# Attention tiles of a hybrid layer: one PSUM row per score tile, one bias-and-minimum pass, one cast and one subtraction, 1/sum moved into the gate

## The chip, the cores and the metric

The kernel runs on one core of one Trainium2 chip. The core has five engines that run their own instruction streams: TensorE (PE; its weight loads are listed apart as PEld), VectorE (DVE), ScalarE (ACT), GpSimd (POOL) and SyncE (SP, which here only issues DMAs). The metric is the time of one execution on the device in microseconds (us). Before the change the median of three runs is 1415.39 us (1412.73 to 1422.43).

## The reference, cut to what matters

One layer over 2048 latent tokens (a grid of 32 rows by 64 columns) and 256 context tokens, width 1024. After a norm and one input projection, half of the width goes through neighbourhood attention (8 heads of 64), the other half through retention (4 heads of 128); both are gated and projected out. The change is in the attention:

```python
s_loc = einsum('bhrqd,bhrkd->bhrqk', qr, kg) * scale + bias     # local window, 8 x 16 keys per query
s_loc = where(mask, s_loc, -inf)
s_ctx = einsum('bhrqd,bhcd->bhrqc', qr, k_ctx) * scale           # 256 context keys, no bias
p = softmax(concatenate([s_loc, s_ctx], axis=-1), axis=-1)       # one softmax over both
o = einsum('bhrqk,bhrkd->bhrqd', p_loc, vg) + einsum('bhrqc,bhcd->bhrqd', p_ctx, v_ctx)
y_na = merge(o) * silu(na_g)
```

All inputs are float32. Products are made in two float32r halves: a value is cast to a high part, and the difference is the low part.

## The kernel before, in words

**Stages.** Until about 560 us the kernel normalises, projects and writes q, k, v and the gates to DRAM scratch (qS, kS, vS, gS). From about 562 to 1062 us run the attention tiles, with the rest of the projection (for the retention) mixed in as filler. Then come the retention's states, scans and the output projection.

**The tiles.** There are 8 heads with 16 tiles each (NT = 128): 4 row blocks i by 4 column blocks j. A tile has 128 queries (8 rows by 16 columns), a window of 12 or 16 rows by 24 or 32 columns of local keys (nk = 288, 384 or 512) and 256 context keys (LC).

**One step of the loop (L958-L1013).** The step t works on three tiles, in this order of issue on all engines:

1. tick() runs deferred stores and other deferred work (L133). A store issued with store() goes out one or more ticks later, in this stage on ACT's DMA queue.
2. s_mm(t): TensorE, four matmuls, local scores into a PSUM tile pl (two buffers), context scores into one half of a PSUM tile pc that two tiles share (L742, L743; order pl, pc, pl, pc).
3. fill(part[0]): filler, one step is 3 or 6 matmuls of the projection (L351, L362). A unit of it ends with an evacuation on ACT and DVE, for the rotary units on DVE with tables that were loaded in the middle of the unit (L405, L435; DVE L412-L414, L448-L450).
4. s_min(t): DVE, context scores copied with a running minimum (L752), then local scores plus bias and minimum in one custom instruction (L754).
5. p_tr(t-2): TensorE transposes 3 or 4 blocks of local and 2 of context weights into PSUM tiles tl and tcx (L773, L776, one buffer each), ACT casts them into pt in two instructions (L778, L779).
6. s_exp(t): ACT, exponential with the sum accumulated (L759). p_lo(t-2): DVE, the low parts in two subtractions (L786, L787). s_norm(t): DVE reciprocal of the sum (L764), POOL multiplies the whole row by it (L765).
7. fill(part[1]), then pv(t-3): TensorE, weights times values into po (L797, L799), and after each second tile combine: ACT copies 64 partitions of po (L817), DVE adds (L818), POOL makes two adds (L821) and, for the last of a row block of an odd head, the product with the gate (L825), which is stored to yS.
8. fill(part[2]), then loads and bias work for later tiles: the bias tiles (POOL, L719, L722), the gate (L807), q of the next row block (L697), values vt in groups of four image rows (L705, 6 buffers), k and context values of the next head (L683, L686).

**What sets the order.** The order is written out by hand; each engine and each DMA queue runs in that order. SP issues all loads of this stage, one after another. A load waits until the buffer that it fills was used for the last time, and all later loads wait behind it. Two halves of one PSUM bank in one tile are not written and read at the same time: the writer waits for the reader.

Of the kernel before, what the change touches and what calls it, by code (L numbers as in the profile page):

```python
# [18 lines left out]
P = 128  # L19
# [57 lines left out]
def hybrid_kernel(ctx: ExitStack, tc: tile.TileContext, a: dict, out: bass.AP):  # L77
# [12 lines left out]
    yS = [dram.tile([KC, P, L // 2], F32, name=f"yS{u}") for u in range(2)]  # L90

# [512 lines left out]
    psl = pool(pax, "psl", 2, space=PSUM)  # L604
    psc = pool(pax, "psc", 1, space=PSUM)

# [73 lines left out]
    def load_head(h):  # L680
        k2 = kp.tile([P, LT], F32R, name="k2")
        for hl in range(2):
            nc.sync.dma_start(f(k2)[64 * hl:64 * hl + 64, :], kS[h // 2][64 * (h % 2):64 * (h % 2) + 64, hl, :])  # L683
        vh = vS[h // 4][:, h % 4, :]
        vc = kp.tile([P, 2, P], F32R, name="vc")
        nc.sync.dma_start(f(vc), vh[L:, :].rearrange("(n p) d -> p n d", p=P))  # L686
        return dict(k2=k2, vh=vh, vc=vc, nb={}, vt={}, q={})

    def load_e(hd, h):
        hd["e"] = kp.tile([P, 16, 32], F32, name="rpbe")  # L690
# [9 lines left out]
    def load_v(hd, gs):  # L700
        for g in gs:
            vt = kp.tile([P, 4, P], F32R, name="vt", bufs=6)
# [10 lines left out]
    def bias(hd, rt, ct):  # L713
# [7 lines left out]
        t = mp.tile([P, kr, cw], F32, name=f"nb{int(rt == 1)}{ct}")  # L721
        nc.gpsimd.tensor_tensor(t, mcol[:, ct, ec:ec + cw].unsqueeze(1).to_broadcast([P, kr, cw]),  # L722
                                hd["ep"][:, :, ec:ec + cw], ALU.subtract)
        hd["nb"][rt, ct] = t
# [7 lines left out]
    def s_mm(t):  # L732
        h, i, j, kr0, kr, kc0, cw = dims(t)
        hd, nk = heads[h], kr * cw
        if t % 2 == 0:
            tl_st["pc"] = psc.tile([P, 2, LC], F32, name="pc")
        pc = tl_st["pc"][:, t % 2, :]
        pl = psl.tile([P, 512], F32, name="pl")
        kg = hd["k2"][:, :L].rearrange("p (r c) -> p r c", c=GW)
        for hl in range(2):  # L740
            qa = hd["q"][i][:, hl, j * P:(j + 1) * P]
            nc.tensor.matmul(pl[:, :nk], qa, kg[:, kr0:kr0 + kr, kc0:kc0 + cw], start=(hl == 0), stop=(hl == 1))  # L742
            nc.tensor.matmul(pc, qa, hd["k2"][:, L:], start=(hl == 0), stop=(hl == 1))  # L743
        sp = ap_.tile([P, 768], F32, name="sp", bufs=3)
        st = ap_.tile([P, 4], F32, name="stt", bufs=4)
        tl_st[t] = dict(pl=pl, pc=pc, sp=sp, st=st, nk=nk)

    def s_min(t):
        h, i, j = dims(t)[:3]
        T = tl_st[t]  # L750
        sp, st, nk = T["sp"], T["st"], T["nk"]
        nc.vector.tensor_scalar(sp[:, nk:nk + LC], T["pc"], 1.0, None, ALU.mult, ALU.min, accum_out=st[:, 0:1])  # L752
        nb = heads[h]["nb"][RTYPE[i], CTYPE[j]].rearrange("p a b -> p (a b)")
        nc.vector.tensor_tensor_reduce(sp[:, :nk], T["pl"][:, :nk], nb, 1.0, st[:, 0:1], ALU.add, ALU.min, st[:, 1:2])  # L754

    def s_exp(t):
        T = tl_st[t]
        sp, st, n = T["sp"], T["st"], T["nk"] + LC
        nc.scalar.activation(sp[:, :n], sp[:, :n], AF.Exp, bias=st[:, 1:2], scale=-1.0, accum_out=st[:, 2:3])  # L759

    def s_norm(t):
        T = tl_st[t]
        sp, st, n = T["sp"], T["st"], T["nk"] + LC
        nc.vector.reciprocal(st[:, 3:4], st[:, 2:3])  # L764
        nc.gpsimd.tensor_scalar(sp[:, :n], sp[:, :n], st[:, 3:4], 0.0, ALU.mult, ALU.add)  # L765

    def p_tr(t):
# [3 lines left out]
        tl = psl.tile([P, 4, P], F32, name="tl", bufs=1)  # L771
        for g in range(ng_):
            nc.tensor.transpose(tl[:cn, g, :], sp[:, g * cn:(g + 1) * cn], ident)  # L773
        tcx = psc.tile([P, 2, P], F32, name="tcx")
        for g in range(2):
            nc.tensor.transpose(tcx[:, g, :], sp[:, nk + g * P:nk + (g + 1) * P], ident)  # L776
        pt = ap_.tile([P, 6, 2, P], F32R, name="pt")
        nc.scalar.copy(pt[:cn, :ng_, 0, :], tl[:cn, :ng_, :])  # L778
        nc.scalar.copy(pt[:, 4:, 0, :], tcx)  # L779
        T.update(tl=tl, tcx=tcx, pt=pt)  # L780

    def p_lo(t):
        h, i, j, kr0, kr, kc0, cw = dims(t)
        T = tl_st[t]
        pt, ng_, cn = T["pt"], kr // 4, 4 * cw
        nc.vector.tensor_tensor(pt[:cn, :ng_, 1, :], T["tl"][:cn, :ng_, :], f(pt)[:cn, :ng_, 0, :], ALU.subtract)  # L786
        nc.vector.tensor_tensor(pt[:, 4:, 1, :], T["tcx"], f(pt)[:, 4:, 0, :], ALU.subtract)  # L787

    def pv(t):
        h, i, j, kr0, kr, kc0, cw = dims(t)  # L790
        T, hd = tl_st[t], heads[h]
        pt, ng_, cn = T["pt"], kr // 4, 4 * cw
# [5 lines left out]
        for g in range(2):  # L798
            nc.tensor.matmul(po[:, t % 2, :, :], hd["vc"][:, g, :], pt[:, 4 + g, :, :], start=False, stop=(g == 1))  # L799
# [4 lines left out]
    def load_gate(t):  # L804
        h, i = dims(t)[:2]
        gts[t // 4] = ap_.tile([P, 512], F32, name="gt")
        nc.sync.dma_start(gts[t // 4], gS[h // 2][:, i * 512:(i + 1) * 512])  # L807

    def combine(t):
# [6 lines left out]
        tmp = ap_.tile([P, 2, 2, P], F32, name="cmb", bufs=1)  # L816
        nc.scalar.copy(tmp[fin], po[oth])  # L817
        nc.vector.tensor_tensor(tmp[fin], po[fin], tmp[fin], ALU.add)  # L818
        yv = ys[i][fin].rearrange("p (r w c) -> p r w c", r=8, w=4)
        for jj in range(2):  # L820
            nc.gpsimd.tensor_tensor(yv[:, :, 2 * jp + jj, :], tmp[fin, jj, 0, :].rearrange("p (r c) -> p r c", r=8),  # L821
                                    tmp[fin, jj, 1, :].rearrange("p (r c) -> p r c", r=8), ALU.add)
        if h % 2 == 1 and jp == 1:
            gt, y2 = gts.pop(t // 4), ys[i]
            nc.gpsimd.tensor_tensor(gt, y2, gt, ALU.mult)  # L825

            y_put(h // 2, i // 2, (i % 2) * 512, gt, 2)
# [522 lines left out]
```

## Time and profile before

| what | us |
|---|---|
| median of 3 runs (lowest, highest) | 1415.39 (1412.73, 1422.43) |
| span of the profiled execution, first to last instruction | 1413.8 |
| PE busy in that span | 1346.2 (95%) |
| DVE / ACT / POOL busy | 670.2 / 553.4 / 614.5 |
| attention stage, 560 to 1062: PE / DVE / ACT / POOL busy | 469.4 / 351.9 / 281.4 / 335.3 |

The page gives for each engine the time in which it had an instruction in work. A row of the view of waits reads: the waiting engine and its line, what it waited for, the total in us, how often, and the longest. A row of the groups reads: line, engine, operation, output and inputs with their shapes, count, then busy us and mean ns of one, then the idle time just before them and what ended it. SPq and ACTq are the DMA issues of SP and ACT.

### The profile page before, as it was taken

The numbers are of one execution on the slowest core, as the hardware profiler recorded it, in microseconds if no ns is written. First come the engines' busy times: TensorE is split into PE (matmuls) and PEld (weight loads), VectorE is DVE, ScalarE is ACT, GpSimd is POOL, SyncE is SP. The second block draws the span as 40 slices with busy tenths as digits, with TensorE's granted clock in tenths as the row PEclk, the third lists the DMA queues.
The fourth block names the chain that finished last, engine by engine and source line by source line (L and its number), as shares of the span: only waits on it lengthen the run. The fifth ranks groups of instructions, "written<-read, shape, count | busy, mean of one in ns | idle before, by whom it ended". The sixth has DMA issues, their size and how long they took to land.

```text
span 1413.8 us, 23044 instructions
## 1 busy us (share of the span) xinstructions
PE 1346.2 (95%) x8380; PEld 1175.6 (83%) x8380; DVE 670.2 (47%) x1563; ACT 553.4 (39%) x1283; POOL 614.5 (43%) x703
## 2 busy tenths in 40 slices
PE   6989999999999999999899988798999999999997
PEld 2467899988887888998799878598999879888886
DVE  5786111100021131677777767577673644344445
ACT  4454212212212221765466544356563234333332
POOL 4452302112201221676777746477673155454342
PEclk9999999999999999999999999999999999999999
DMA  9543666233244577557557585847436997555433
GB/s 310 168 164 133 215 219 231 92 110 104 90 147 159 202 266 218 141 156 196 158 155 174 162 241 167 227 124 191 134 115 203 295 310 258 188 168 174 154 117 127
DMA packets 203634, 253.20 MB, mean 179 GB/s; under 512 B 13057, under 2 KB 151425, under 8 KB 202498
## 3 DMA queue, kind: packets, MB, share of 16 engines
q1 hardware_dynamic: 168098, 186.98, 45.2%
q10 hardware_dynamic: 35424, 64.76, 12.7%
q8 instruction: 66, 1.08, 0.3%
q14 instruction: 46, 0.38, 0.1%
HBM read 168.86 MB, written 82.84 MB: 178 GB/s over the span
## 4 chain that ended last, share of the span: by engine, by line
PE 73%; DMA 10%; DVE 8%; ACT 3%; POOL 2%; issue 2%; SPq 1%; ACTq 0%; DVEq 0%; POOLq 0%
PE mm L351 24%; PE mm L362 19%; PE mm L1193 11%; PE po L797 2%; PE tl L773 2%; PE pl L742 2%; PE mm L916 2%; DMA t<-in_rot_s_dram 2%; DMA q<-qS 2%; PE pc L743 1%; PE po L799 1%; PE tcx L776 1%; PE mm L295 1%; DMA t<-in_rot_k_dram 1%; PE mm L1105 1%
## 5 line engine op out<-in xcount | busy, mean ns | idle before, releaser
L351 PE MATMUL mm<-hhi,whi 128*128 128x512 f32 x640 | 259.6, 406 | 0.0
L351 PE MATMUL mm<-hlo,whi 128*128 128x512 f32 x640 | 253.4, 396 | 5.6 <-DVE hlo L264 2.2
L351 PE MATMUL mm<-hhi,wlo 128*128 128x512 f32 x640 | 253.3, 396 | 0.3 <-DVE wlo L332 0.3
L362 PE MATMUL mm<-whi,hhi 128*128 128x256 f32 x768 | 224.6, 292 | 0.0
L362 PE MATMUL mm<-wlo,hhi 128*128 128x256 f32 x768 | 216.7, 282 | 2.7 <-POOL wlo L332 2.7
L362 PE MATMUL mm<-whi,hlo 128*128 128x256 f32 x768 | 216.1, 281 | 0.0
L332 POOL TENSOR_TENSOR wlo<-st,whi 128x256 fp32r<-128x256 f32 (+1 forms) x97 | 112.4, 1176 | 225.4 <-ACT whi L330 225.2
L765 POOL TENSOR_SCALAR sp<-sp,stt 128x640 f32<-128x640 f32 (+2 forms) x128 | 103.6, 810 | 105.4 <-DVE stt L764 79.6
L362 PEld LDWEIGHTS mm<-wlo,hhi 128*128 128x128 f32 x768 | 145.0, 189 | 3.4 <-POOL wlo L332 3.3
L351 PEld LDWEIGHTS mm<-hlo,whi 128*128 128x128 f32 x640 | 120.8, 189 | 31.3 <-issue 3.3
L362 PEld LDWEIGHTS mm<-whi,hhi 128*128 128x128 f32 x768 | 145.2, 189 | 1.1
L362 PEld LDWEIGHTS mm<-whi,hlo 128*128 128x128 f32 x768 | 145.3, 189 | 0.0
L351 PEld LDWEIGHTS mm<-hhi,whi 128*128 128x128 f32 x640 | 120.9, 189 | 29.1 <-issue 4.6
L351 PEld LDWEIGHTS mm<-hhi,wlo 128*128 128x128 f32 x640 | 120.5, 188 | 29.4 <-DVE wlo L332 0.7
L759 ACT ACTIVATE sp<-sp,stt 128x640 f32<-128x640 f32 (+2 forms) x128 | 107.9, 843 | 51.8 <-DVE stt L754 51.3
L778 ACT CAST pt<-tl 96x384 fp32r<-96x384 f32 (+3 forms) x128 | 67.9, 531 | 150.6 <-PE tl L773 137.2
L786 DVE TENSOR_TENSOR pt<-tl,pt 96x384 fp32r<-96x384 f32 (+3 forms) x128 | 79.4, 620 | 44.5 <-ACT pt L778 43.8
L1193 PE MATMUL mm<-wor,y 128*128 128x512 f32 x384 | 95.6, 398 | 1.5 <-DVE xt L1202 1.1
L742 PE MATMUL pl<-k,q 128*128 128x384 f32 (+2 forms) x256 | 83.3, 346 | 7.1 <-DMA q<-qS 7.1
L1193 PE MATMUL mm<-won,y 128*128 128x512 f32 x336 | 89.9, 406 | 0.0
L743 PE MATMUL pc<-k,q 128*128 128x256 f32 x256 | 72.1, 286 | 16.8 <-DVE sp L752 16.7
L1193 PEld LDWEIGHTS mm<-wor,y 128*128 128x128 f32 x384 | 69.9, 188 | 17.7 <-issue 3.4
(220 smaller groups left out, 2639.1 us busy)
## 6 DMA issues: line engine op xcount, KB each, us to landing
st<-in_w_in_dram SPq DMA_DIRECT2D x48, 512.0 KB
q<-qS SPq DMA_DIRECT2D x64, 256.0 KB
vS<-o ACTq DMA_DIRECT2D x18, 512.0 KB
k<-kS SPq DMA_DIRECT2D x16, 576.0 KB
kS<-o SPq DMA_DIRECT2D x16, 512.0 KB
woS<-g ACTq DMA_DIRECT2D x32, 256.0 KB
qS<-o ACTq DMA_DIRECT2D x16, 512.0 KB
vt<-vS SPq DMA_DIRECT2D x128, 64.0 KB
```

The lines of the kernel that those rows point to most:

```text
L332: eng.tensor_tensor(l, r, f(h), ALU.subtract)
L351: nc.tensor.matmul(pm[:, :n], ww[:, k, cs], h[:, k, :], start=(k == 0 and i == 0), stop=(k == KC - 1 and i == 2))
L362: nc.tensor.matmul(pm[:, t * WG:(t + 1) * WG], h[:, k, o:o + P], ww[:, k, :], start=(k == 0 and i == 0), stop=(k == KC - 1 and i == 2))
L742: nc.tensor.matmul(pl[:, :nk], qa, kg[:, kr0:kr0 + kr, kc0:kc0 + cw], start=(hl == 0), stop=(hl == 1))
L743: nc.tensor.matmul(pc, qa, hd["k2"][:, L:], start=(hl == 0), stop=(hl == 1))
L759: nc.scalar.activation(sp[:, :n], sp[:, :n], AF.Exp, bias=st[:, 1:2], scale=-1.0, accum_out=st[:, 2:3])
L765: nc.gpsimd.tensor_scalar(sp[:, :n], sp[:, :n], st[:, 3:4], 0.0, ALU.mult, ALU.add)
L773: nc.tensor.transpose(tl[:cn, g, :], sp[:, g * cn:(g + 1) * cn], ident)
L778: nc.scalar.copy(pt[:cn, :ng_, 0, :], tl[:cn, :ng_, :])
L786: nc.vector.tensor_tensor(pt[:cn, :ng_, 1, :], T["tl"][:cn, :ng_, :], f(pt)[:cn, :ng_, 0, :], ALU.subtract)
L797: nc.tensor.matmul(po[:, t % 2, :, :], hd["vt"][kr0 // 4 + g][:cn, j, :], pt[:cn, g, :, :], start=(g == 0), stop=False)
L1193: nc.tensor.matmul(pm, yy[:, k, :], ww[:, k, sl], start=(k == 0 and i == 0), stop=(k == 3 and i == 2))
```

## The change

- The scores of a tile lie in one row of a PSUM tile sS of three banks that is never handed out anew: an even tile has its local scores at the end of the first bank and its context scores in the first half of the second, an odd tile its context scores in the second half of the second bank and its local scores in the third. The two local matmuls are issued first, then the two for the context.
- The bias lies in two rows with 256 zeros between the pieces, so one custom instruction over nk + 256 elements adds the bias, takes the minimum and writes SBUF; L752 goes.
- All transposes of a tile go into one PSUM tile tr of two banks; one cast and one subtraction replace two each. The window of the pipeline is one step shorter: p_tr and p_lo work on t-1, pv and combine on t-2; the loop runs NT+2 steps.
- The row is not multiplied by 1/sum (L764, L765 go). The sums of the four tiles of a row block go into one 128x4 tile; after the fourth, one reciprocal is taken and stored to DRAM scratch rS, transposed (one 4-byte element at a time). For odd heads, three steps later, SP loads the gate and, twice, a row of rS spread over 64 partitions; three steps after that POOL multiplies the gate by it and y by the gate, and y is stored.
- combine: ACT copies half as many elements (64x256), two DVE adds replace one DVE add of 64x512 and two POOL adds.
- Buffers: vt 7 instead of 6, sp 2 instead of 3, one instead of two for the gate and the relative bias.

```diff
+    sS = psc.tile([P, 3 * 512], F32, name="sS")
+    tr = psc.tile([P, 6, P], F32, name="tr")
...
-            vt = kp.tile([P, 4, P], F32R, name="vt", bufs=6)
+            vt = kp.tile([P, 4, P], F32R, name="vt", bufs=7)
...
+        pl = sS[:, 1024:1024 + nk] if odd else sS[:, 512 - nk:512]
+        pc = sS[:, 768:1024] if odd else sS[:, 512:768]
...
+        for o, k in ((pl, kg[:, kr0:kr0 + kr, kc0:kc0 + cw]), (pc, hd["k2"][:, L:])):
+            for hl in range(2):
+                nc.tensor.matmul(o, hd["q"][i][:, hl, j * P:(j + 1) * P], k, start=(hl == 0), stop=(hl == 1))
...
-        nc.vector.tensor_scalar(sp[:, nk:nk + LC], T["pc"], 1.0, None, ALU.mult, ALU.min, accum_out=st[:, 0:1])
-        nc.vector.tensor_tensor_reduce(sp[:, :nk], T["pl"][:, :nk], nb, 1.0, st[:, 0:1], ALU.add, ALU.min, st[:, 1:2])
+        nc.vector.tensor_tensor_reduce(T["sp"][:, :n], T["s"], nbz[big][:, o:o + n], 1.0, 3e38, ALU.add, ALU.min, T["st"])
...
-        nc.vector.reciprocal(st[:, 3:4], st[:, 2:3])
-        nc.gpsimd.tensor_scalar(sp[:, :n], sp[:, :n], st[:, 3:4], 0.0, ALU.mult, ALU.add)
...
+    def r_put(t):
+        h, i = dims(t)[:2]
+        r = heads[h]["r"][i]
+        nc.vector.reciprocal(r, r)
+        store(rS[h][i].rearrange("j q -> q j"), r)
...
-        nc.scalar.copy(pt[:cn, :ng_, 0, :], tl[:cn, :ng_, :])
-        nc.scalar.copy(pt[:, 4:, 0, :], tcx)
+        nc.scalar.copy(pt[:, :ng_ + 2, 0, :], tr[:, :ng_ + 2, :])
...
-        nc.vector.tensor_tensor(pt[:cn, :ng_, 1, :], T["tl"][:cn, :ng_, :], f(pt)[:cn, :ng_, 0, :], ALU.subtract)
-        nc.vector.tensor_tensor(pt[:, 4:, 1, :], T["tcx"], f(pt)[:, 4:, 0, :], ALU.subtract)
+        nc.vector.tensor_tensor(pt[:, :n, 1, :], tr[:, :n, :], f(pt)[:, :n, 0, :], ALU.subtract)
...
+        nc.scalar.copy(tmp[fin], po[oth, :, 0, :])
+        nc.vector.tensor_tensor(tmp[fin], po[fin, :, 0, :], tmp[fin], ALU.add)
+        nc.vector.tensor_tensor(yv, po[fin, :, 1, :].rearrange("p j (r c) -> p j r c", r=8),
+                                tmp[fin].rearrange("p j (r c) -> p j r c", r=8), ALU.add)
...
+    def r_load(t):
+        rb = ap_.tile([P, 512], F32, name="rb", bufs=1)
+        for e in range(2):
+            nc.sync.dma_start(rb[64 * e:64 * e + 64, :], rS[h - 1 + e][i].rearrange("j q -> (j q)").unsqueeze(0).to_broadcast([64, 512]))
...
+    def gate_put(t):
+        nc.gpsimd.tensor_tensor(gv, gv, rb.rearrange("p (w r c) -> p w r c", r=8, w=4), ALU.mult)
+        nc.gpsimd.tensor_tensor(y2, y2, gt, ALU.mult)
+        y_put(h // 2, i // 2, (i % 2) * 512, y2, 2)
...
-    for t in range(NT + 3):
+    for t in range(NT + 2):
...
+        if 0 < t <= NT and t % 4 == 0:
+            r_put(t - 1)
+            if dims(t - 1)[0] % 2 == 1:
+                defer(3, lambda t=t: (load_gate(t - 1), r_load(t - 1)))
+                defer(6, lambda t=t: gate_put(t - 1))
+        if 0 <= t - 1 < NT:
+            p_tr(t - 1)
```

109 lines of the change are left out of this document (49 added, 60 removed).

## The prediction

> **What bounds the kernel now.** I read the page first, then the busy time by stretch, then the waits of TensorE in the attention stage, and from there who held those it waited for.
>
> ```profile
> span 1413.8 us, 23044 instructions
> PE 1346.2 (95%) x8380; PEld 1175.6 (83%) x8380; DVE 670.2 (47%) x1563; ACT 553.4 (39%) x1283; POOL 614.5 (43%) x703
> 560.00:1062.00 502.00, 469.38 (x3494) 442.01 (x3493) 351.85 (x1040) 281.36 (x669) 335.26 (x447) 0.99 0.62 168
> 1062.00:1120.00 58.00, 57.66 (x425) 53.92 (x425) 28.15 (x74) 16.57 (x33) 16.34 (x19) 1.00 0.79 249
> ```
>
> The row of the stretch 560 to 1062 gives the busy time of PE, PEld, DVE, ACT and POOL, then the granted clock, the DMA share and GB/s. PE is busy in 469.4 of 502 us. The change leaves TensorE its matmuls and transposes, so it can give back at most the 32.6 us in which PE stood, and 0.01 of 502, some 5 us, that the lower clock took. DVE, ACT and POOL have 30 to 44% of the stage free: taking work from them gains nothing by itself.
>
> ```profile
> PE pc L743 <- DVE sp L752: 16.7, 6, 8.0
> PE pl L742 <- DMA q<-qS: 7.1, 5, 2.7
> PE tl L773 <- DVE pt L786: 5.7, 4, 3.8
> PE po L797 <- DVE cmb L818: 2.2, 6, 0.7
> DVE o L412 <- DMA t<-in_rot_s_dram: 13.2, 3, 8.3
> DVE o L448 <- DMA t<-in_rot_k_dram: 9.6, 3, 5.3
> ACT whi L330 <- DMA st<-in_w_in_dram: 6.9, 1, 6.9
> SPq L705 <- PE po L799: 84.8, 20, 8.4
> SPq L807 <- DMA yS<-gt: 14.3, 5, 5.0
> ```
>
> These are waits inside the stage. PE's largest, 16.7 us, names DVE, yet DVE has time: it stands itself 22.8 us in the filler's evacuations for rotary tables. The 7.1 us are q loads; the longest tl wait (3.8) hangs on ACT, which waited 6.9 us for a weight load. So most of PE's idle time is loads that come late. SP issues them in order, and it stands 84.8 us in front of vt loads whose buffer pv still reads. The longest stall shows it:
>
> ```profile
> 908.18 0.40 PE L742 MATMUL pl<-k,q 128*128 128x512 f32 x1
> 916.61 0.58 PE L743 MATMUL pc<-k,q 128*128 128x256 f32 x1 [8.03 <-DVE sp L752]
> 916.99 0.63 PE L742 MATMUL pl<-k,q 128*128 128x512 f32 x1
> 914.11 0.69 DVE L412 TENSOR_TENSOR o<-mm,t 64x512 f32<-64x512 f32 x1 [8.34 <-DMA t<-in_rot_s_dram]
> 894.35 4.59 SPq L705 DMA_DIRECT2D vt<-vS  x4
> 904.05 0.33 SPq L405 DMA_DIRECT2D t<-in_rot_s_dram  x1
> ```
>
> DVE was ready at 914.11 - 8.34 = 905.8; the table was issued at 904.05 and came ten us later. Until it came, DVE could not read the scores, and PE could not write pc, whose bank DVE had still to read. After the stall the same matmul takes 0.63 instead of 0.40 us, the lowered clock.
>
> **The change part by part: work off the path.** These groups are of the stage.
>
> ```profile
> L752 DVE TENSOR_SCALAR_CACHE_REDUCE sp<-pc 128x256 f32<-128x256 f32 x128 | 53.6, 419 | 23.1 <-PE pc L743 17.2 <-POOL nb L722 2.2 <-POOL sp L765 1.1
> L754 DVE CUSTOM_DVE_ANT_0 sp<-pl,nb,stt 128x512 f32<-128x512 f32 x32 | 24.0, 751 | 1.1
> L754 DVE CUSTOM_DVE_ANT_0 sp<-pl,nb,stt 128x288 f32<-128x288 f32 x32 | 16.6, 518 | 1.3 <-DVE sp L752 0.2
> L787 DVE TENSOR_TENSOR pt<-tcx,pt 128x256 fp32r<-128x256 f32 x126 | 51.9, 412 | 0.0
> L786 DVE TENSOR_TENSOR pt<-tl,pt 128x512 fp32r<-128x512 f32 x32 | 22.0, 689 | 10.6 <-ACT pt L778 10.6
> L764 DVE RECIPROCAL stt<-stt 128x1 f32<-128x1 f32 x128 | 21.0, 164 | 21.0 <-ACT sp L759 16.3
> L818 DVE TENSOR_TENSOR cmb<-po,cmb 64x512 f32<-64x512 f32 x62 | 42.7, 688 | 30.1 <-ACT cmb L817 30.0
> L779 ACT CAST pt<-tcx 128x256 fp32r<-128x256 f32 x127 | 47.7, 375 | 0.0
> L778 ACT CAST pt<-tl 128x512 fp32r<-128x512 f32 x32 | 18.8, 586 | 40.8 <-PE tl L773 39.2 <-PE tcx L776 1.4
> L821 POOL TENSOR_TENSOR y<-cmb 64x128 f32<-64x128 f32 x124 | 54.4, 458 | 13.9 <-DVE cmb L818 12.8
> L765 POOL TENSOR_SCALAR sp<-sp,stt 128x640 f32<-128x640 f32 x64 | 51.4, 803 | 49.5 <-DVE stt L764 44.8 <-PE pc L743 3.8 <-PE tl L773 0.4
> L825 POOL TENSOR_TENSOR gt<-y,gt 128x512 f32<-128x512 f32 x15 | 19.4, 1291 | 1.2
> ```
>
> The custom pass costs (751 - 518) / (512 - 288) = 1.04 ns an element, so 256 more add 0.27 us where L752 took 0.42: 0.15 x 128 = 20 us off DVE. Joining two subtractions saves one fixed part: (689 - 412) / 256 = 1.08 ns an element leaves 0.41 - 0.28 = 0.13 us, times 128, 17 us. Reciprocals go from 128 to 32: 16 us. Two adds of 64x256 at about 0.41 instead of one of 0.69 cost 64 x 0.13 = 8 us more. DVE: about -45. ACT's cast: (586 - 375) / 256 = 0.82 ns an element, so joining saves 0.375 - 0.21 = 0.16 us, 21 us, and the half copy a little more. POOL loses L765 (some 0.80 x 128 = 103 us) and L821 (54), and gains a second product of 1.3 us sixteen times (21; its strided view may cost up to twice that). All this counts as nothing in the sum, because PE's work covers it; without that cover the largest, DVE, would be worth 45 us.
>
> **On the path: the loads.** With pv one step earlier and a seventh vt buffer, a group of image rows takes a buffer whose readers ended long ago, in nearly all cases: the 84.8 us of holds go. Mean hold 84.8 / 20 = 4.2 us, longest 8.4. What SP issues behind a hold moves ahead by about that; q's buffer still ties SP to within a step of PE. With 4.2 us, the q stalls vanish (7.1, longest 2.7), the 8.0 us stall keeps 3.8, the other pc stalls behind tables vanish. About 2 us of the 16.7 I leave, since two short ones are DVE's own queue: 16.7 - 2 - 3.8 = 10.9. The weight load behind the tl stall comes 4.2 earlier: 3.8. Together 7.1 + 10.9 + 3.8 = 21.8 us. Bounds: nothing, if the transfers and not their issue are late; 29.5 (16.7 + 7.1 + 5.7), if all go. The clock goes with the stalls: 21.8 / 32.6 of 5 is 3.3 (0 to 5).
>
> **On the path: the shorter pipeline.** The exponential of tile t now has to end before the transposes in the next step, where it had one step more and a POOL pass. One tile of before:
>
> ```profile
> 873.05 0.28 PE L743 MATMUL pc<-k,q 128*128 128x256 f32 x1
> 875.08 0.62 DVE L754 CUSTOM_DVE_ANT_0 sp<-pl,nb,stt 128x384 f32<-128x384 f32 x1
> 875.74 0.83 ACT L759 ACTIVATE sp<-sp,stt 128x640 f32<-128x640 f32 x1 [0.53 <-DVE stt L754]
> 876.48 0.18 ACT L759 ACTIVATION_READ_ACCUMULATOR sp<-sp,stt 128x1 f32 x1
> 877.74 0.49 PE L773 MATMUL tl<-ident,sp 128*96 128x128 f32 x3
> ```
>
> Scores done at 873.33, exponential done at 876.66, the next step's transposes at 877.74: 1.1 us to spare, and the joined pass adds 0.15. Where a rotary evacuation and a combine fall into one step, DVE comes later by more than that. Of some 36 rotary units I let a third fall so, at 0.2 us: 2 us lost. Below nothing it cannot go; the upper end is the rival below. Waiting behind a late exponential are the transposes, then pv, the next scores and all filler.
>
> pc of the next tile still shares its bank with pc of this one, and the reader is now the whole pass: 0.42 + 0.27 + (512 elements at most) ends up to 0.6 us later than L752 did, while a pl matmul more stands ahead. In the six waits of L743 that is at most 3.6 us; I take 1.5. The Trainium skill, PSUM — Partial Sum Buffer, section "PSUM bank collisions raise a hardware error", says that two engines may not touch one bank of the same partitions at the same time, whichever columns; the row of L743 agrees, and by the rule the wait would not go away with the new layout.
>
> **On the path: new DMAs.** Sixteen times two loads of 128 KB on SP, and 32 stores of 512 elements of 4 bytes on ACT's queue.
>
> ```profile
> q1 hardware_dynamic: 55714, 68.66, 52.5%
> DMA packets 66870, 83.75 MB, mean 168 GB/s; under 512 B 4556, under 2 KB 51840, under 8 KB 65920
> 1071.96 0.40 ACTq L143 DMA_DIRECT2D yS<-gt  x1
> 1072.40 0.51 ACT L910 ACTIVATE vw<-v,w 128x256 f32<-128x256 f32 x1 [3.54 <-POOL gt L825]
> ```
>
> 4.2 MB more at 0.62 x 502 / 83.75 = 3.7 us a MB are 16 us of the rings. An element packet isn't shown: nothing at the low end, at the high end the mean of queue 1, 0.525 x 502 x 16 / 55714 = 76 ns, so 16384 x 76 / 16 = 78 us. The share goes from 0.62 to 0.65 or to 0.81. I take the low end, 4 bytes being far from the mean 1.2 KB, and 3 us for loads that take longer (0 to 15). The Trainium skill, DMA: Bandwidth & Descriptors, section "Rules for kernel authors", speaks against this store: a last dimension that isn't contiguous becomes one descriptor per element, and should be rearranged. No row of before shows such a store; by the rule the high end would hold, and the sum be up to 12 us higher. ACT issues it in about 0.4 us, within its free time. SP waits for the store before the spread row, but no longer 14.3 us for the gate's buffer (y is stored now): I set one against the other.
>
> At the end, ACT stood until 1071.96 for the last yS store and went on 0.4 us later, with PE in filler all along (57.7 of 58 us). Now that store waits for the round trip of the sums: store, spread load, two POOL products. One step fewer in the pipeline (3 us) pays for it. Zero, -2 to +4. The two memsets before the loop lie beside the last projection units: zero.
>
> **The sum.** -21.8 - 3.3 + 2 + 1.5 + 3 = -18.6. From the span, 1413.8 - 18.6 = 1395.2. The span is 1.6 below the median of the runs, which I add as what lies around it: 1396.8, so 1397, 1.3% below 1415.39. A measurement of this kernel tells about 1% from no change.
>
> **The rivals.** First, the rings are the limit: that the table of 904.05 took ten us speaks for it, and the stretch has transfers of k and of spilled activations in flight then; against it, SP's holds come before most stalls. Then holds become longer flights and about a quarter of the 25.1 is gained: -6.3 + 6.5, 1415.6. By the Trainium skill's rule on element descriptors it would come out here too. Second, all late loads are cured, pipeline costs nothing: -29.5 - 5 = -34.5, 1381. For it: only one stall (8.0) is longer than the longest hold that a load is freed from plus PE's own lead, so SP's issue could cure each; against: the ten us of flight. Third, slower: the exponential misses the transposes in most tiles, because the cast of t-1 stands ahead of it on ACT and DVE's single subtraction waits for that cast. It decides from the point where DVE or ACT falls 1.25 us further behind than in the tile shown. At 0.3 us a tile, 128 x 0.3 = 38, against a gain of 18.6 + 2: 1413.8 + 1.6 + 38 - 20.6 = 1433. For it: spare time of only 1.1; against: DVE and ACT both get shorter.
>
> **How the numbers follow.** Forecast 0.47, first rival 0.28, second 0.12, third 0.13. The forecast's own range, 1388 to 1406, lies mostly past the 1% mark of 1401.2; with the second rival that gives faster 0.55. Same: the first rival and the forecast's weak end, 0.32. Slower 0.13. The range takes in the second rival and the first, 1379 to 1418, and leaves out the third and the far ends.
>
> **What would show it.** Right: waits of SP's vt loads for pv near zero; PE's q, pc and tl waits in the stage near 10 us in sum, the largest below 5; DVE near 305 and POOL near 200 busy in the stage; transposes hardly waiting for ACT. Wrong: rotary tables that still come late though SP issued them early (the rings); transposes waiting for the exponential in tens of steps; SP standing for the store of the sums.

## The result and the profile after

The change makes the kernel slower: 1567.15 us (median; 1562.70 to 1570.06) against 1418.37 us for the kernel before on the same chip, a ratio of 1.1055, 95% interval 1.1016 to 1.1093. The forecast was 1397 with a range up to 1418, so even the third rival (1433) was far too low. Lines of the page after: the span, busy times, packets, queue 10 (ACT's DMA queue), and the chain that ended last.

```profile
span 1567.3 us, 22341 instructions
PE 1388.5 (89%) x8380; PEld 1211.7 (77%) x8380; DVE 629.1 (40%) x1148; ACT 530.4 (34%) x1155; POOL 478.7 (31%) x467
DMA packets 223086, 257.44 MB, mean 164 GB/s; under 512 B 30466, under 2 KB 168834, under 8 KB 221955
q10 hardware_dynamic: 52320, 64.83, 12.6%
PE 54%; DMA 31%; DVE 5%; issue 3%; SPq 2%; POOL 2%; ACT 2%; ACTq 0%; POOLq 0%; DVEq 0%
PE mm L352 22%; PE mm L363 11%; PE mm L1210 10%; DMA rS<-rr 8%; DMA vt<-vS 7%; DMA rkS<-o 3%; DMA q<-qS 3%; PE mm L932 2%; DMA t<-in_rot_k_dram 2%; DMA gt<-gS 2%; DMA st<-in_w_in_dram 1%; PE mm L296 1%; SPq L717 1%; DMA v<-rvS 1%; DMA k<-kS 1%
```

DVE and POOL work less, as intended, and PE has the same 8380 matmuls. Yet DMA is 31% of the chain instead of 10%, and its first row is the new store of the sums, `rS<-rr`. The queues of the kernel before, from its page:

```profile
q1 hardware_dynamic: 168098, 186.98, 45.2%
q10 hardware_dynamic: 35424, 64.76, 12.7%
```

Queue 10 carries 52,320 packets where it had 35,424. Its packets take 12.6% of a span of 1567.3 us, which is 198 us of the 16 engines, where they took 12.7% of 1413.8, or 180: by the durations of its own packets, the stores cost some 18 of the 149 us. The stretches show what it does cost. Columns: the stretch and its length, busy PE, PEld, DVE, ACT, POOL, granted clock, DMA share, GB/s.

```profile
560.00:1200.00 640.00, 508.35 (x3479) 475.56 (x3479) 309.22 (x622) 257.52 (x539) 196.48 (x208) 0.90 0.68 136
612.00:617.00 5.00, 5.00 (x44) 5.00 (x43) 1.88 (x5) 1.54 (x3) 0.81 (x1) 1.00 0.65 174
617.00:619.00 2.00, 2.00 (x18) 2.00 (x17) 0.82 (x1) 1.87 (x4) 0.00 (x0) 1.00 0.38 89
619.00:628.00 9.00, 3.57 (x28) 3.17 (x26) 1.57 (x4) 1.10 (x4) 1.43 (x2) 0.92 0.27 30
628.00:633.00 5.00, 2.32 (x11) 2.35 (x12) 1.72 (x4) 3.50 (x8) 2.86 (x4) 0.50 0.35 104
```

The attention stage now runs from 560 to some 1200, 640 us instead of 502, at 136 instead of 168 GB/s. The four short stretches are one store, issued at 616.67. Before it, 174 GB/s; then for nine us 30 GB/s with a DMA share of 0.27. In these nine us the profile calls the DMA engines mostly idle, though loads that had been issued had not landed, as the rows of the timeline round that store show:

```profile
614.70 8.78 SPq L717 DMA_DIRECT2D vt<-vS  x8
616.67 0.37 ACTq L144 DMA_DIRECT2D rS<-rr  x1
619.72 0.41 ACT L331 CAST whi<-st 128x256 fp32r<-128x256 f32 x1
628.15 0.37 ACTq L144 DMA_DIRECT2D rvS<-o  x1
628.55 0.40 ACT L331 CAST whi<-st 128x256 fp32r<-128x256 f32 x1 [8.43 <-DMA vt<-vS]
629.71 0.83 DVE L794 TENSOR_TENSOR pt<-tr,pt 128x640 fp32r<-128x640 f32 x1 [8.25 <-ACT pt L788]
630.68 0.66 PE L784 MATMUL tr<-ident,sp 128*128 128x128 f32 x2 [7.70 <-DVE pt L794]
```

SP issued eight vt loads from 614.70 on. ACT did its work up to 619.72 + 0.41 = 620.1 and then stood at the issue of its next DMA (628.15) until a vt load had landed. With ACT stood the cast (L788), with it DVE's subtraction, and with that TensorE, for 7.7 us. This store is one of the worse ones. Taken at each of the 32 stores, the same view gives a mean of 186 GB/s in the 5 us before the issue and of 60 GB/s from 4 to 12 us after it, there at a DMA share of 0.61: on the whole the engines are not idle but carry a third of the bytes.

The waits of the stage (560 to 1230) show where such stalls ended; columns: total us, times, longest.

```profile
PEld tr L784 <- ACT sp L769: 60.4, 22, 8.1
PE tr L784 <- DVE pt L794: 52.9, 18, 7.9
PE sS L752 <- DMA q<-qS: 24.3, 5, 9.1
PE po L804 <- DMA vt<-vS: 15.8, 5, 4.4
PE mm L932 <- ACT vw L926: 11.3, 1, 11.3
SPq L834 <- DMA rS<-rr: 57.5, 11, 10.0
SPq L717 <- DMA rS<-rr: 17.9, 5, 9.5
```

Everything that comes by DMA is late: q, vt, the weights that ACT casts. The first two rows are the transposes, which wait for ACT's exponential and for the subtraction behind its cast, both late with ACT. SP, too, now stands 57.5 us for the store of the sums before it spreads them (L834). The granted clock is lower too: 0.50 in the last short stretch, after TensorE had stood, and 0.90 in the whole stage where it was 0.99.

### The profile page after: what moved, and what is told of

It is laid out like the page before. It is cut to its first block, busy times and chain, and to the rows that moved or that the text cites. A ratio compares the mean times of both kernels' runs of the same rounds, so it can differ in the third digit from the quotient of the medians.

```text
span 1567.3 us, 22341 instructions
## 1 busy us (share of the span) xinstructions
PE 1388.5 (89%) x8380; PEld 1211.7 (77%) x8380; DVE 629.1 (40%) x1148; ACT 530.4 (34%) x1155; POOL 478.7 (31%) x467
## 3 DMA queue, kind: packets, MB, share of 16 engines
q10 hardware_dynamic: 52320, 64.83, 12.6%
## 4 chain that ended last, share of the span: by engine, by line
PE 54%; DMA 31%; DVE 5%; issue 3%; SPq 2%; POOL 2%; ACT 2%; ACTq 0%; POOLq 0%; DVEq 0%
PE mm L352 22%; PE mm L363 11%; PE mm L1210 10%; DMA rS<-rr 8%; DMA vt<-vS 7%; DMA rkS<-o 3%; DMA q<-qS 3%; PE mm L932 2%; DMA t<-in_rot_k_dram 2%; DMA gt<-gS 2%; DMA st<-in_w_in_dram 1%; PE mm L296 1%; SPq L717 1%; DMA v<-rvS 1%; DMA k<-kS 1%
## 5 line engine op out<-in xcount | busy, mean ns | idle before, releaser
L363 PE MATMUL mm<-whi,hhi 128*128 128x256 f32 x768 | 229.9, 299 | 0.0
L788 ACT CAST pt<-tr 128x640 fp32r<-128x640 f32 (+1 forms) x128 | 95.6, 747 | 294.0 <-PE tr L786 180.6
L794 DVE TENSOR_TENSOR pt<-tr,pt 128x640 fp32r<-128x640 f32 (+1 forms) x128 | 113.8, 889 | 202.3 <-ACT pt L788 200.4
L363 PEld LDWEIGHTS mm<-whi,hhi 128*128 128x128 f32 x768 | 150.3, 196 | 0.0
L752 PE MATMUL sS<-k,q 128*128 128x256 f32 (+3 forms) x512 | 105.7, 331 | 41.1 <-DMA q<-qS 24.3
L784 PE MATMUL tr<-ident,sp 128*128 128x128 f32 (+1 forms) x448 | 77.5, 294 | 63.6 <-DVE pt L794 52.9
L761 DVE CUSTOM_DVE_ANT_0 sp<-sS,nb 128x640 f32<-128x640 f32 (+2 forms) x128 | 105.8, 827 | 67.1 <-PE sS L752 63.1
L752 PEld LDWEIGHTS sS<-k,q 128*128 128x128 f32 x512 | 89.8, 202 | 49.6 <-issue 31.8
L784 PEld LDWEIGHTS tr<-ident,sp 128*128 128x128 f32 (+1 forms) x448 | 55.6, 143 | 75.8 <-ACT sp L769 60.4
L804 PE MATMUL po<-pt,vt 128*128 128x256 f32 (+1 forms) x448 | 81.3, 299 | 28.2 <-DMA vt<-vS 15.8
```

Of the source, the lines that this page charges most:

```text
L363: nc.tensor.matmul(pm[:, t * WG:(t + 1) * WG], h[:, k, o:o + P], ww[:, k, :], start=(k == 0 and i == 0), stop=(k == KC - 1 and i == 2))
L752: nc.tensor.matmul(o, hd["q"][i][:, hl, j * P:(j + 1) * P], k, start=(hl == 0), stop=(hl == 1))
L761: nc.vector.tensor_tensor_reduce(T["sp"][:, :n], T["s"], nbz[big][:, o:o + n], 1.0, 3e38, ALU.add, ALU.min, T["st"])
L784: nc.tensor.transpose(tr[:cn, g, :], sp[:, T["lo"] + g * cn:T["lo"] + (g + 1) * cn], ident)
L788: nc.scalar.copy(pt[:, :ng_ + 2, 0, :], tr[:, :ng_ + 2, :])
L794: nc.vector.tensor_tensor(pt[:, :n, 1, :], tr[:, :n, :], f(pt)[:, :n, 0, :], ALU.subtract)
```

## The experiments

Times are medians; the ratio is to the kernel before on the same chip (1417.0 to 1418.8), with its 95% interval.

| run | us | ratio | interval |
|---|---|---|---|
| no_round_trip | 1412.05 | 0.9956 | 0.9939 to 0.9973 |
| before_plus_store | 1556.13 | 1.0967 | 1.0935 to 1.0998 |
| rows_by_transpose | 1438.27 | 1.0129 | 1.0093 to 1.0164 |
| before_vt7 | 1406.68 | 0.9911 | 0.9882 to 0.9940 |
| pieces_of_16 | 1428.34 | 1.0085 | 1.0054 to 1.0116 |
| store_from_sp | 1544.94 | 1.0896 | 1.0863 to 1.0930 |
| longer | 1405.36 | 0.9916 | 0.9885 to 0.9947 |
| old_norm | 1412.60 | 0.9956 | 0.9933 to 0.9978 |
| spaced_elements | 1417.85 | 1.0007 | 0.9981 to 1.0032 |
| quarter_elements | 1516.91 | 1.0688 | 1.0652 to 1.0723 |
| pieces_512x16 | 1421.60 | 1.0021 | 1.0002 to 1.0040 |
| pieces_128x16 | 1417.90 | 0.9996 | 0.9976 to 1.0017 |
| elements_16_apart | 1421.72 | 1.0018 | 0.9998 to 1.0038 |
| pieces_128x8 | 1428.93 | 1.0082 | 1.0055 to 1.0108 |
| vt7_early_tables | 1413.46 | 0.9974 | 0.9957 to 0.9991 |
| pieces_16_early_tables | 1425.44 | 1.0055 | 1.0034 to 1.0076 |

### Is it the store?

Theory A: the stores of single elements hold up all transfers. Rivals: the shorter pipeline (B), and SP standing for the loads that spread the sums (C).

**no_round_trip**, the change without the store of the sums and the loads that spread them; the gate is multiplied by itself instead, so the division by the sum is left out.

```diff
-        store(rS[h][i].rearrange("j q -> q j"), r)
-            nc.sync.dma_start(rb[64 * e:64 * e + 64, :], rS[h - 1 + e][i]...to_broadcast([64, 512]))
-        nc.gpsimd.tensor_tensor(gv, gv, rb.rearrange(...), ALU.mult)
+        nc.gpsimd.tensor_tensor(gv, gv, gv, ALU.mult)
```

> The changed kernel without the way of the sums through DRAM: no store of rS, no load of rb; the gate is multiplied by itself in place of 1/sum, so the division by the sum is left out; everything else as changed. Theory A (the stores of 512 single 4-byte elements hold up the DMA engines, and all loads and stores behind them come late): about 1400, between 1385 and 1425. Theory B (the pipeline that is one step shorter: the transposes wait for the exponential and for the cast): stays above 1530. Theory C (SP stands for the spread loads and so issues everything else late): also about 1400, so this run parts B from A and C.

**before_plus_store**, the kernel before with the 32 stores alone; nothing reads them.

```diff
+        if 0 < t <= NT and t % 4 == 0:
+            nc.vector.tensor_copy(rr, tl_st[t - 1]["st"])
+            store(rS[(t - 1) // 16][(t - 1) // 4 % 4].rearrange("j q -> q j"), rr)
```

> The kernel before, which has the longer pipeline, plus 32 stores of a 128x4 tile to DRAM, transposed one 4-byte element at a time, from ACT's queue at the same steps as in the changed kernel; nothing reads them. Theory A: 1500 to 1570, most of the loss in one small edit. Theory B and theory C: within 10 us of before, 1412 to 1428, since neither the pipeline nor any load on SP changes.

**rows_by_transpose**, the change with the sums transposed by TensorE and stored as four rows of 512 bytes (the combine adds in place, to make room).

```diff
-        store(rS[h][i].rearrange("j q -> q j"), r)
+        nc.tensor.transpose(sS[0:4, 1024:1024 + P], r, ident)
+        nc.vector.tensor_copy(rt4, sS[0:4, 1024:1024 + P])
+        store(rS[h][i], rt4)
```

> The changed kernel, with the four sums of a row block transposed by TensorE into a free bank, copied by DVE and stored as four rows of 512 bytes; the spread loads and all waits for them stay. (To make room, combine adds in place in y.) Theory A: about 1400, between 1385 and 1425. Theory B: above 1530. Theory C: above 1500, since SP still waits for the round trip. With the run without the round trip this parts C from A.

**before_vt7**, the kernel before with the seventh vt buffer alone.

```diff
-            vt = kp.tile([P, 4, P], F32R, name="vt", bufs=6)
+            vt = kp.tile([P, 4, P], F32R, name="vt", bufs=7)
-        hd["e"] = kp.tile([P, 16, 32], F32, name="rpbe")
+        hd["e"] = kp.tile([P, 16, 32], F32, name="rpbe", bufs=1)
```

> The kernel before with a seventh buffer for vt (and one instead of two for the relative bias, to make room): the term of the prediction by which SP's holds go. If a load that is freed from its hold also lands earlier in time, as predicted: 10 to 20 us faster, 1398 to 1408. If the transfers are late whatever SP does: within 5 us of before.

Without the round trip the change takes 1412 us; the kernel before with the bare store takes 1556, 137 more than without it. So the store is nearly all of the loss: 137 of 149 us, 4.3 us a store. The stretch 560 to 1060 of before_plus_store, which is the old code otherwise:

```profile
560.00:1060.00 500.00, 390.21 (x2636) 363.85 (x2635) 278.11 (x829) 211.10 (x502) 254.24 (x337) 0.88 0.68 135
```

In the same stretch the changed kernel has 139 GB/s and a clock of 0.89, and the kernel before 168 and 0.99: the loss is there without any of the new layout. Other loads are carried more slowly, too. Queue 1 has the packets and bytes of the kernel before, and they take 47.4% of 1552.9 us, 736 us of the engines, where they took 45.2% of 1413.8, or 639:

```profile
q1 hardware_dynamic: 168098, 186.98, 47.4%
```

That no_round_trip is fast with the shorter pipeline refutes B. C is bounded: rows_by_transpose still has the spread loads and their waits, where C foresaw more than 1500. At 1438 it also lies 13 us above A's range and 26 above no_round_trip. A good part of these 26 seems to be its own transposes, which wait for DVE's reciprocal, as its waits from 560 to 1200 show:

```profile
PE sS L778 <- DVE rr L776: 29.2, 19, 5.6
```

### Is it the issuer, the number of pieces, or their size?

**pieces_of_16**, the change with the sums stored as they lie, 128 pieces of 16 bytes a store; the product with the gate reads them in that order.

```diff
-        store(rS[h][i].rearrange("j q -> q j"), r)
+        store(rS[h][i], r)
-  rb.rearrange("p (w r c) -> p w r c", r=8, w=4)
+  rb.rearrange("p (r c w) -> p w r c", r=8, w=4)
```

> The changed kernel with the sums stored as they lie in SBUF, 128 pieces of 16 bytes in a store in place of 512 of 4, and read back by the product in that order; the loads spread the same 2 KB rows. Theory A1, a store costs by its pieces: 32 element stores cost 138 us on the kernel before, 4.3 us each, so a quarter is 1.1 us each and 34 us in all; on top of the 1412 without the round trip that is 1446, and up to 10 more for the loads. Theory A2, a scattered address costs, not the piece (element q of row j lay 512 bytes from that of the next row): the pieces are now one contiguous 2 KB run, and the time is 1412 to 1425. Theory A3, any store out of 128 partitions costs the same: 1550 or more.

**store_from_sp**, before_plus_store with SP as the issuer.

```diff
-            store(rS[...].rearrange("j q -> q j"), rr)
+            defer(1, lambda t=t, rr=rr: nc.sync.dma_start(rS[...].rearrange("j q -> q j"), rr))
```

> The kernel before with the same 32 element stores as in the earlier run (1556), issued by SP in place of ACT; nothing reads them. Theory D, the engines that move data are what is held up: no difference by issuer, 1530 to 1570. Theory E, it is ACT that stands at its next issue until the lane comes free, and its casts and exponentials with it: with ACT out of it more than half of the 138 us goes, 1430 to 1490.

SP as the issuer gives 1545 instead of 1556: 128 of the 137 us stay. So D holds: what ACT does while it stands at its next issue is how the stall travels in one place, not its cause. pieces_of_16 at 1428 lay just above A2's range and well below A1's 1446: a quarter of the pieces cost far less than a quarter. Four bare stores on the kernel before then took number, size and place apart; their edits are shown against before_plus_store.

**spaced_elements**: 512 elements of 4 bytes, each alone in 64 bytes of the target.

```diff
-    rS = [dram.tile([4, 4, P], F32, ...
+    rS = [dram.tile([4, 4, P, 16], F32, ...
-            store(rS[...].rearrange("j q -> q j"), rr)
+            store(rS[...][:, :, 0].rearrange("j q -> q j"), rr)
```

> The kernel before with 32 stores of 512 elements of 4 bytes from ACT's queue, as in the run of 1556, but with each element alone in 64 bytes of its target; nothing reads them. Theory N, the number of pieces costs: again 130 to 145 over the kernel before, 1545 to 1565. Theory M, small neighbours that share a line of the target hold each other up: under 40 over it, below 1455.

**quarter_elements**: 128 elements, adjacent.

```diff
-            store(rS[...].rearrange("j q -> q j"), rr)
+            store(rS[...][0:1].rearrange("j q -> q j"), rr[:, 0:1])
```

> The kernel before with 32 stores of 128 elements of 4 bytes (one column of the four), 4 bytes apart in the target; nothing reads them. Theory N with a fixed price a piece (138 us / 16384 = 8.4 ns): 35 over the kernel before, about 1452. Theory N2, pieces cost only from some number a store on, which 128 doesn't reach: 0 to 15 over it, 1417 to 1432. Theory M: a quarter of the neighbours, 35 as well.

**pieces_512x16**: the number of pieces of the change, 16 bytes each.

```diff
-            store(rS[...].rearrange("j q -> q j"), rr)
+            store(rS[...].rearrange("j q c -> q j c"), ident[:, 0:16].rearrange("q (j c) -> q j c", j=4))   # target [4, 4, P, 4]
```

> The kernel before with 32 stores of 512 pieces of 16 bytes from ACT's queue (constants; nothing reads them): the number of pieces of the change's store with the size of those in the run with 16-byte pieces. Theory N and N2, the number decides: 1545 to 1565. Theory S, the size decides (4 bytes are dear, 16 not): at most four times what 128 such pieces cost, so 1417 to 1475.

**pieces_128x16**: the store of pieces_of_16 on the kernel before.

```diff
-            store(rS[...].rearrange("j q -> q j"), rr)
+            store(rS[...], rr)                                        # target [4, P, 4]
```

> The kernel before with 32 stores of 128 pieces of 16 bytes from ACT's queue, nothing reads them. The round trip with such a store cost 16 us over the kernel without it (1428 against 1412). If the store is most of that: 10 to 16 over the kernel before, 1427 to 1433. If the loads that spread the rows and SP's wait for the store are: 0 to 5, 1417 to 1422. At 8.4 ns a piece, theory N: 1452.

The number of pieces is refuted as the price. The same 16384 elements, 64 bytes apart, cost nothing (ratio 1.0007), and a quarter of them, adjacent, cost 98 us, far above what any of the three theories expected there (at most 1452). Queue 10 has 52,320 packets in spaced_elements, as many as after the change, and 40,032 in quarter_elements. The stretch 560 to 1060 of spaced_elements, and then of quarter_elements:

```profile
560.00:1060.00 500.00, 466.44 (x3456) 438.71 (x3455) 359.02 (x1064) 279.21 (x663) 332.61 (x443) 0.98 0.64 167
```

```profile
560.00:1060.00 500.00, 417.32 (x2868) 384.50 (x2866) 305.48 (x905) 229.57 (x546) 280.45 (x370) 0.92 0.67 146
```

167 against 146 GB/s, with more packets where it is faster. From 4 to 12 us after a store's issue, the mean over the 32 stores is 152 GB/s in spaced_elements and 85 in quarter_elements. The size of 16 bytes is harmless, 512 or 128 of them: +3 and 0 us.

**elements_16_apart**: 512 elements, four to 64 bytes, none to share 16 bytes. **pieces_128x8**: 128 adjacent pieces of 8 bytes.

```diff
-            store(rS[...].rearrange("j q -> q j"), rr)
+            store(rS[...][:, :, 0].rearrange("j q -> q j"), rr)      # target [4, 4, P, 4]
...
+            store(rS[...], rr[:, 0:2])                                # target [4, P, 2]
```

> The kernel before with 32 stores of 512 elements of 4 bytes from ACT's queue, 16 bytes apart in the target, so four share 64 bytes; nothing reads them. Theory M1, elements that share 64 bytes hold each other up, each after the one before: a cost of some 24 ns an element as with 128 adjacent ones (98 us / 32 / 128), 100 us or more over the kernel before. Theory M2, only those that share 16 bytes do: 0 to 5 over it, 1417 to 1424.

> The kernel before with 32 stores of 128 adjacent pieces of 8 bytes; nothing reads them. Two of them share 16 bytes and eight share 64. Theory M2: two share where four did with 4 bytes, so a third to a half of the 98 us of 128 adjacent elements, 1450 to 1470. Theory M1: eight share where sixteen did, about half, 1455 to 1475. A theory by size, 4 bytes alone are dear: 1417 to 1424.

Elements 16 bytes apart cost 0.2% (interval 0 to 0.4), so sharing 64 bytes isn't it (M1 falls). Adjacent pieces of 8 bytes cost 12 us (0.8%): less than M1 and M2 expected, more than the theory by size, so none of the three ranges held. Pieces of 16 bytes cost nothing there, and adjacent 4-byte elements 98. What fits all rows: pieces that share 16 bytes of the target hold the transfers up, four to 16 bytes far more than two. Another rule fits them as well and no run parts the two: every store with a clear cost here has pieces that begin off a multiple of 16 bytes from the start of its target, and the others have none. Lone elements that begin there would tell. Why the price is so steep, and in which part of the chip the pieces wait, stays open too. The place where it is felt is shown: the transfers of the core, as in the 60 GB/s above.

### Where did the predicted gain stay?

no_round_trip gains 6 us by its ratio; the seventh buffer alone gains 12. So the rest of the change, without its round trip, costs some 6 us more than it brings. Two runs part it.

**longer**: no_round_trip with transposes and pv each one step later, as before (the division is left out here too). To make room, the combine adds in place; sp has three buffers again.

```diff
-    for t in range(NT + 2):
+    for t in range(NT + 3):
-            p_tr(t - 1)
+            p_tr(t - 2)
-            pv(t - 2)
+            pv(t - 3)
```

> The kernel without the round trip (1412; the division by the sums is left out), with the transposes and the product with v each one step later, as before the change; to make room the combine adds in place. Theory F, the shorter pipeline is where the 5 us against the kernel before with seven buffers (1407) went: 1400 to 1407. Theory G, late rotary tables stall VectorE, whatever the pipeline: 1409 to 1415.

**old_norm**: longer with the old division, so the change without its 1/sum part and its shorter pipeline.

```diff
+        nc.vector.reciprocal(st[:, 2:3], st[:, 1:2])
+        nc.gpsimd.tensor_scalar(sp[:, :n], sp[:, :n], st[:, 2:3], 0.0, ALU.mult, ALU.add)
-        nc.gpsimd.tensor_tensor(gv, gv, gv, ALU.mult)
```

> The run named longer with the old division: a reciprocal on VectorE and a product on GpSimd for each tile, nothing multiplied into the gate but y. So it is the change without its last part, and with the longer pipeline. If the division of before lies beside TensorE's work: within 4 us of the run named longer, 1400 to 1415, and the change without the 1/sum part is worth 0 to 1%. If GpSimd's and VectorE's extra 115 us come into the path: 1420 to 1450.

**vt7_early_tables** and **pieces_16_early_tables**: before_vt7 and pieces_of_16 with the rotary tables issued two parts of a filler unit sooner.

```diff
-        pm, n, tok = yield from mid(g, 3, load) if ct == 0 else g
+        pm, n, tok = yield from mid(g, 1, load) if ct == 0 else g
-        pm = yield from mid(g, 2, load) if tp < 8 else g
+        pm = yield from mid(g, 0, load) if tp < 8 else g
```

> The kernel before with seven vt buffers (1407), and the rotary tables issued after the first part of the k units (not the third) and after the second part of the q units (not the fourth). If late tables make the stalls that are left: 1398 to 1403, and no wait of TensorE over 3 us that goes back to a table. If the tables then wait for their buffers or for other loads: 1404 to 1412.

> The changed kernel with the sums stored in pieces of 16 bytes (1428), and the rotary tables issued earlier in the same way. If late tables make its stalls: 1417 to 1422. If the round trip of the sums and SP's waits do: 1425 to 1430.

From run to run, by medians: before_vt7 1406.7; old_norm 1412.6, so the joined row with its new combine, its single gate buffer and its later gate load costs 6 us; longer 1405.4, so the division of each tile is worth 7 us, where its expectation had at most 4; no_round_trip 1412.1, so the shorter pipeline, with the sp buffer and the form of the combine in which longer differs as well, costs 7 (theory F; its expected 1400 to 1407 held). The runs are from two chips; by the ratios the steps are 6 each. Each of these three steps has intervals that overlap at their ends; the signs are likely, the sizes good to a few us. A wait that bears on the joined row is TensorE's for the bank that VectorE still reads, 11.4 us in before_vt7 (below) and in old_norm:

```profile
PE sS L752 <- DVE stt L761: 21.6, 6, 8.5
```

The profiled executions of the two are equally long, 1408.0 and 1408.3 us, so what this wait makes of the 6 us stays open. The waits of no_round_trip, 560 to 1062, and its longest stall:

```profile
SPq L813 <- POOL y L839: 27.4, 9, 5.9
SPq L709 <- PE sS L752: 17.0, 7, 7.6
SPq L717 <- PE po L805: 9.3, 3, 3.2
PEld tr L783 <- ACT sp L769: 5.8, 3, 3.3
PE po L803 <- DVE y L826: 9.8, 4, 5.5
PE sS L752 <- DVE stt L761: 6.6, 3, 4.4
```

```profile
885.97 0.38 SPq L436 DMA_DIRECT2D t<-in_rot_k_dram  x1
895.18 0.42 DVE L449 TENSOR_TENSOR o<-mm,t 128x256 f32<-128x256 f32 x1 [5.91 <-DMA t<-in_rot_k_dram]
897.66 1.20 PE L803 MATMUL po<-pt,vt 96*128 96x256 f32 x4 [5.49 <-DVE y L826]
```

A rotary table takes nine us to come, ten in the kernel before, and DVE stands with everything behind it. The early tables were to show whether an earlier issue cures that. vt7_early_tables is 7 us slower than before_vt7, above both of its expected ranges. Waits of TensorE and SP, before_vt7 and then vt7_early_tables (560 to 1062):

```profile
PE pc L743 <- DVE sp L752: 11.4, 5, 4.8
PE pl L742 <- DMA q<-qS: 2.7, 2, 2.1
SPq L705 <- PE po L799: 25.7, 9, 5.5
SPq L697 <- PE pc L743: 14.2, 7, 4.2
SPq L435 <- DVE o L413: 11.0, 3, 4.7
SPq L405 <- DVE sp L752: 4.0, 3, 3.0
```

```profile
PE pl L742 <- DMA q<-qS: 11.2, 5, 5.6
PE pc L743 <- DVE sp L752: 4.4, 3, 2.2
SPq L435 <- DVE o L413: 17.1, 3, 11.3
SPq L405 <- DVE sp L752: 9.5, 4, 4.7
```

TensorE's waits behind VectorE shrank by 7 us and those for q loads grew by 8.5. But the edit was a poor test of an earlier issue: the table comes earlier in SP's order, yet SP then stands 11.6 us longer for the table's buffer (L435, L405), with the q loads behind it, and VectorE still stood 12.2 us for tables, 8.2 in before_vt7. Whether the loads also slow each other in flight, these runs don't tell. On pieces_of_16 the same edit is worth about 3 us by the medians, as the rival there expected.

before_vt7, at 0.9911 of the kernel before, is the fastest version here that does the whole computation, and the one to keep.

## Why the prediction was wrong

**The step that failed is "On the path: new DMAs", +3 us with bounds of 0 and 15.** It was wrong in size by 150 us, and by the way it was priced. The view it rested on, what packets take as a share of the rings, cannot hold this cost: with the stores, queue 10's own packets took 18 us more, while the transfers of the core fell after them from 186 to 60 GB/s in the mean. "4 bytes being far from the mean 1.2 KB" argued from size to price, and for neighbours of 4 bytes it goes the other way. Also the high end (78 us of ring time, turned into a share of 0.81) wasn't a bound on anything but ring time. The measured terms are 137 for the stores (before_plus_store) and, with stores that cost nothing, about 16 for the spread loads and SP's wait (pieces_of_16 less no_round_trip, with pieces_128x16 at 0), where 3 was said for all of it. With the 6 us that no_round_trip gains, -6 + 137 + 16 = 147 of the 149 us. SP stood for those sums in pieces_of_16 from 555 to 1230:

```profile
SPq L834 <- DMA rS<-rr: 21.0, 8, 6.2
```

"I set one against the other" (the hold for the store against the old 14.3 us for the gate's buffer) was therefore wrong as well: SP stands for both, the gate's load for 27.4 us in no_round_trip.

**The warning that was taken for 12 us.** The Trainium skill, DMA: Bandwidth & Descriptors, section "Rules for kernel authors", was right to advise against this store, and the prediction should have taken the warning for more than 12 us. But one descriptor per element isn't what cost here: spaced_elements has as many and costs nothing. The Trainium skill, same page, section "Why small descriptors are slow (HBM only)", charges each packet and each descriptor a fixed overhead; by that, spaced and adjacent elements would cost alike, and the runs with 1.0007 and 1.0967 say otherwise. Nor does the prediction's price of the rule lead to the first rival's 1415.6, as it says there: 12 us on 1397 are 1409.

**The late loads, -21.8 and -3.3.** The hold did go: SP's wait for pv fell from 84.8 us to 9.3 in no_round_trip. What was wrong is that "what SP issues behind a hold moves ahead by about that". Of the gain that was to follow, the seventh buffer gives 12 on the kernel before, within its bounds. One reason why no more is in SP's rows of before_vt7: its hold for pv falls to 25.7, but its stand for q's buffer is 14.2 where it was 2.1, and that for a table's buffer 11.0 where it was 1.7, so what one hold frees is in part taken by the next. In no_round_trip these two are 17.0 and 13.0. The other is the flight, nine us for a table; that was the first rival's mechanism, and how the two share what is missing stays open. About half of the gain came where that rival had a quarter. Its price for the whole (1415.6) is off as well, for it too had the stores cost a few us.

**The shorter pipeline and the joined row, +2 and +1.5.** Both had the right sign and were too small: 7 and 6 us, as far as runs whose intervals overlap can say, and each with more than its term in it. The mechanism named for the pipeline, an evacuation and a combine in one step, is seen in the stalls of L803 above, where it holds pv and not the transposes that the prediction named; that the late table then stands in front of the combine was the part left out.

**Work off the path, "nothing".** The durations came out or were better: at the prediction's 1.04 ns an element, the custom pass over 640 elements would take 751 + 128 x 1.04 = 884 ns, and it took 818; the single subtraction would take 689 + 128 x 1.08 = 827 ns, and took 823.

```profile
L761 DVE CUSTOM_DVE_ANT_0 sp<-sS,nb 128x640 f32<-128x640 f32 x64 | 52.4, 818 | 44.9 <-PE sS L752 43.1 <-POOL wlo L333 1.1 <-POOL gt L841 0.2
L794 DVE TENSOR_TENSOR pt<-tr,pt 128x640 fp32r<-128x640 f32 x64 | 52.6, 823 | 100.7 <-ACT pt L788 100.4
```

DVE at 309 and POOL at 196 busy in the stage are close to the 305 and 200 foretold. That the division of each tile is worth nothing is doubtful: longer and old_norm differ by 7 us.

**The tail, zero, -2 to +4.** The last store waited for the round trip, as said, but a step fewer did not pay for it: TensorE stood 11.3 us for ACT's vw (the row of L932 above), and ACT for the stores of y. With stores that cost nothing the same wait is 4.1 us in pieces_of_16, the upper end said, but it is 4.2 in before_vt7 too, which has no round trip.

**The third rival** (1433, the exponential misses the transposes) had the right side and, after the change, its sign: transposes wait for the exponential 22 times, 60.4 us. But its reason was ACT's and DVE's own order of work, and that was the same in no_round_trip, where the row has 3 times and 5.8 us. The exponential was late because ACT stood for a DMA. So all three signs that the prediction named against itself showed after the change; the other two are SP standing for the store of the sums (57.5 us) and late tables (VectorE stood 23.2 us for those of the k units), though by then the stores held up every load.

## What to carry to other kernels

Don't store single 4-byte elements side by side to DRAM from many partitions; write each partition's run of 16 bytes or more as it lies, and let the reader undo the order, which here cost POOL another view: 1.55 instead of 1.29 us a product, sixteen times, off the path. An operation that no row shows has no upper bound from the rows of other operations: try it alone on the old kernel first, as before_plus_store did. And the durations of a store's own packets don't tell what it holds up: compare the GB/s of the core in the ten us after it with those before, and the time that the packets of the other queues take.

## What the runs showed of the hardware

- 32 stores of 512 adjacent 4-byte elements cost 137 us, 128 of them a store 98 us, which is 24 ns an element and 3.1 us a store; the same 512 elements 16 or 64 bytes apart cost 0 to 0.4% and nothing; pieces of 16 bytes nothing to 0.4%, 128 adjacent pieces of 8 bytes 0.8%.
- After such a store the transfers of the core slow down: a mean of 60 GB/s from 4 to 12 us after the issue, at a DMA share of 0.61, where spaced_elements has 152 at 0.55. After one store it was 30 GB/s at a share of 0.27 for nine us. The loads' own packets take longer: queue 1's, the same in number and bytes, 736 instead of 639 us of the engines in before_plus_store.
- By whom it is issued matters little: 1545 us from SP, 1556 from ACT. But an engine that computes and issues DMAs, as ACT does here, stands with all its work at its next issue, 8.4 us in the row shown, for a load that SP had issued.
